# Opening of a three-block sequence model: x loaded half of its columns at a time on two queues, the norm's weight rows in a group of their own, and the norm's split parts made from the transposes in six banks

## The chip, the cores and the metric

One core of a Trainium2 chip (trn2) runs the kernel. The metric is the device time in microseconds (us), the median of several runs. A profile of one execution, taken by the hardware profiler, shows what each engine did: TensorE (PE, with its weight loads as PEld), VectorE (DVE), ScalarE (ACT), GpSimd (POOL), and SyncE (SP), which here only issues DMAs.

## The reference, cut to what matters

Three blocks in a row work on x of 512 tokens by 1024 features in float32. The change lies at the start of the first:

```python
def rmsnorm(x, w):
    xf = x.astype(jnp.float32)
    y = xf * lax.rsqrt(jnp.mean(xf * xf, axis=-1, keepdims=True) + EPS)
    return (y * w.astype(jnp.float32)).astype(x.dtype)

h = rmsnorm(x, norm_mix_w[l])
proj = h @ w_in[l]          # split into the inputs of an SSM and a gated delta-rule mixer
...
x = x + merged @ w_out[l]
h = rmsnorm(x, norm_ffn_w[l])
gate, up = jnp.split(h @ w_ffn_in[l], [FFN_HIDDEN], axis=-1)
x = x + (jax.nn.silu(gate) * up) @ w_ffn_down[l]
```

The other two blocks (attention and recurrent mixers, feed-forward networks) are not touched.

## The kernel before, in words

Data lie in two ways: FM tiles hold 128 features on the partitions and the 512 tokens along the free dimension, TM tiles hold 128 tokens on the partitions. x comes in TM from DRAM and is needed in FM, as eight tiles. A float32 product is made of three products of split parts (`mm3`, L215 to L218): a high part `wh` or `hi` that ScalarE casts (L194), and a low part `wl` or `lo`, the rest, that VectorE subtracts (L195). Weights come in pieces of 512 KB through three raw buffers (`wr`) on SP's queue (L210).

The opening does this. `setup_consts` (L95 on) makes masks and the identity on VectorE from two index tiles of GpSimd (`ident` at L109; L118 is the last that reads both index tiles), and zeros a tile (L127) that is stored four times into DRAM areas (`blocks`, 256 KB and a small rest each, L132 and L133). Its scratch are tiles of the tag `tmp`, of which there are six: two index tiles, two made from these, two for the masks; the zeros are the seventh and take the slot of the first. `first_block` then loads x with `load_fm` (eight banks of transposes, copied into FM tiles by VectorE and ScalarE in turn, L365), loads vectors of per-feature weights as rows and transposes them into columns (`columns`, L138), among them the norm's weight, and calls `norm`. For each of the eight feature blocks `norm` scales x by the norm's weight into a high part (ScalarE, L322) and a low part (VectorE, L323), squares x (ScalarE, L325) and adds the squares up (VectorE, L327). After the last, TensorE sums over features (L282, in `token_sums`), VectorE finds the reciprocal root (L180 to L189, copied into `r` at L330), and TensorE spreads it over the partitions (L293, in `spread`). The first products of the input projection (32 columns of `dt` and of gates in `lin_small`, then two pieces of 128 columns) start from the parts that lack the root, and are multiplied by it afterwards; all that follows uses the whole norm, made by `whole`.

The order in which each engine runs is not that of the code. A framework orders the instructions of each engine when the program is built, by its own estimate of when each is ready, and puts the waits in; on the chip an engine then goes through its list in that order. A slot of a tag is given out again when the last reader of the tile before is done. Each DMA signals one of eight semaphores in turn, one set for SP's and ACT's DMAs together and one for POOL's, so a DMA is not issued before the one eight places before it in its set has landed.

Of the kernel before, what the change touches and what calls it, by code (L numbers as in the profile page):

```python
# [11 lines left out]
F32 = mybir.dt.float32  # L12
# [4 lines left out]
AF = mybir.ActivationFunctionType  # L17
# [3 lines left out]
P = 128  # L21
# [11 lines left out]
class Env:  # L33
    """Pools, constants and the pieces that the blocks share.

    FM tiles hold features on partitions and the 512 tokens along the free
    dimension; TM tiles hold 128 tokens on partitions."""
# [14 lines left out]
    @contextmanager  # L52
    def on(self, stream):
        """Tiles inside come from the slots of a scan's stream ("a" or "b"): slots of one tag
        are given out in program order, so work that is to run side by side has its own."""
        kept, self.stream = self.stream, stream
        yield
        self.stream = kept
# [79 lines left out]
    def columns(self, parts):  # L138
        """Vectors whose elements belong to features, as columns: parts is a
        list of (name, AP of [rows, 128]); gives name -> [128, rows] APs."""  # L140
# [3 lines left out]
        def flush():  # L144
            rows = self.tmp()[:, :P]
            at = 0
            for _, ap, r in group:
                nc.gpsimd.dma_start(rows[at:at + r, :], ap)
                at += r
# [19 lines left out]
    def bcast_load(self, ap1d, n):  # L169
        """A vector of n elements, on every partition."""  # L170
# [4 lines left out]
    def rsqrt(self, ss, n, scale, eps):  # L175
        """(ss * scale + eps) ** -0.5 on a [128, n] piece; eps a number or such a piece."""
# [15 lines left out]
    def split(self, src, hi, lo):  # L192
        """src as the exact sum of two float32r parts."""
# [3 lines left out]
    def parts(self, src):  # L197
        """The two parts of src in tiles of their own."""
# [4 lines left out]
    def weights(self, w, k0, nk, c0, nf):  # L203
        """Rows k0*128.. (nk blocks) and columns c0..c0+nf of w [K, F], split."""
# [15 lines left out]
    def lin_fm(self, w, c0, ncols, h, epi, k0=0, nk=KB):  # L220
        """epi(i, psum) for each 128 columns of x @ w[:, c0:c0+ncols], FM."""
# [10 lines left out]
    def lin_tm(self, w, c0, h, epi, ncols=S):  # L232
        """epi(c, g, psum) for each 128 tokens and each 256 columns of x @ w[:, c0:c0+ncols], TM."""
# [17 lines left out]
    def lin_small(self, w, pieces, h):  # L251
        """The few columns of pieces, (first, number) each, FM: psum [columns, 512]."""
# [15 lines left out]
    def to_tm(self, fm, r0, nf):  # L268
        """Rows r0..r0+nf of an FM tile, TM: psum [128 tokens, 4, nf]."""
# [7 lines left out]
    def token_sums(self, acc):  # L277
        """acc: FM [128, 512] already summed over feature blocks; psum [128 tokens, 4] with the
        sums over all features."""
# [5 lines left out]
    def token_rstd(self, acc, scale, eps):  # L285
        """The reciprocal root of the sums of acc, in a psum bank, on all partitions."""
# [1618 lines left out]
```

## Time and profile before

| what | us |
|---|---|
| time, median of 3 runs | 3030.83 |
| lowest and highest run | 3030.61, 3033.38 |
| span of the profiled execution | 3028.6 |
| TensorE busy in it | 2947.4 (97%) |
| VectorE busy | 1735.4 (57%) |
| ScalarE busy | 1112.4 (37%) |

The span runs from the first to the last instruction of the profiled execution. What lies around it is not in the profile: the median of the runs is 2.2 us above this span. Busy time is that of matrix products on TensorE, of computing instructions on the others; the issue of a DMA is not counted. Idle time of an engine that does not hold up the others costs nothing.

### The profile page before, as it was taken

The page shows a single profiled execution, that of the slowest core. Times are in us where ns is not written, and L with a number is a line of the kernel's source. Part 1 is how long each engine was busy: PE and PEld are TensorE (multiplying, and loading weights), DVE is VectorE, ACT ScalarE, POOL GpSimd, SP SyncE. Part 2 cuts the span into 40 slices and gives each one's busy share as a digit, 9 for nine tenths or more (in the row PEclk, how much of TensorE's full clock was granted, in tenths as well). Part 3 has the DMA queues.
Part 4 walks back from the last instruction along what each step waited for, and adds up shares of the span by engine and source line. Part 5 has one row for each costly group of instructions (what it writes and reads, how often), then busy time and mean ns, then how long its engine had stood idle before and what let it go on. Part 6 is the DMA issues. An engine that isn't in the chain of part 4 may idle for free. (4 is left out here: it accounts for less than half of the span.)

```text
span 3028.6 us, 39369 instructions
## 1 busy us (share of the span) xinstructions
PE 2947.4 (97%) x15170; PEld 2430.1 (80%) x15170; DVE 1735.4 (57%) x3871; ACT 1112.4 (37%) x2076; POOL 46.9 (2%) x95
## 2 busy tenths in 40 slices
PE   6999999999999999999999999999999999999999
PEld 4778888888788886788978878888987978888887
DVE  6787737655655457977653564333757563553343
ACT  4435424433322233333253332222465553332221
POOL 1000000000000000000000000000000000000000
PEclk9999999999999998999999999999999999999999
DMA  5222233233445322222113423333321214333332
GB/s 125 78 58 77 60 96 98 68 97 98 139 144 162 91 84 85 71 59 58 34 32 87 131 83 92 98 97 102 118 70 57 63 44 131 98 91 96 99 91 90
DMA packets 481660, 269.06 MB, mean 89 GB/s; under 512 B 30607, under 2 KB 469073, under 8 KB 481473
## 3 DMA queue, kind: packets, MB, share of 16 engines
q1 hardware_dynamic: 445680, 255.67, 28.9%
q10 hardware_dynamic: 33920, 9.44, 1.3%
q0 software_dynamic: 1872, 1.43, 0.6%
q8 instruction: 120, 1.97, 0.3%
q14 instruction: 68, 0.55, 0.1%
HBM read 252.20 MB, written 14.16 MB: 88 GB/s over the span
## 5 line engine op out<-in xcount | busy, mean ns | idle before, releaser
L194 ACT CAST wh<-wr 128x1024 fp32r<-128x1024 f32 (+3 forms) x447 | 454.0, 1016 | 1293.0 <-PE pl L217 914.3
L216 PE MATMUL pl<-h,wh 128*128 128x512 f32 x2224 | 878.8, 395 | 10.0 <-DVE long L1186 4.6
L218 PE MATMUL pl<-h,wl 128*128 128x512 f32 x2224 | 875.7, 394 | 11.5 <-DVE wl L195 11.5
L217 PE MATMUL pl<-h,wh 128*128 128x512 f32 x2224 | 878.0, 395 | 1.0 <-DVE h L195 1.0
L195 DVE TENSOR_TENSOR wl<-wr,wh 128x1024 fp32r<-128x1024 f32 (+3 forms) x447 | 525.9, 1177 | 413.3 <-ACT wh L194 402.0
L216 PEld LDWEIGHTS pl<-h,wh 128*128 128x128 f32 x2224 | 419.8, 189 | 100.6 <-DVE long L1186 5.4
L218 PEld LDWEIGHTS pl<-h,wl 128*128 128x128 f32 x2224 | 419.2, 189 | 100.9 <-DVE wl L195 14.8
L217 PEld LDWEIGHTS pl<-h,wh 128*128 128x128 f32 x2224 | 419.5, 189 | 90.3 <-issue 3.5
L217 PE MATMUL pl<-long,wh 128*128 128x512 f32 x648 | 252.9, 390 | 0.2 <-DVE long L195 0.2
L216 PE MATMUL pl<-long,wh 128*128 128x512 f32 x648 | 253.1, 391 | 0.0
L218 PE MATMUL pl<-long,wl 128*128 128x512 f32 x648 | 253.0, 390 | 0.0
L543 DVE SCALAR_TENSOR_TENSOR long<-pl,long 128x512 f32<-128x512 f32 x72 | 49.8, 691 | 178.3 <-PE pl L218 178.3
L216 PEld LDWEIGHTS pl<-long,wh 128*128 128x128 f32 x648 | 121.7, 188 | 26.3 <-issue 1.0
L218 PEld LDWEIGHTS pl<-long,wl 128*128 128x128 f32 x648 | 121.7, 188 | 25.6 <-issue 0.3
L217 PEld LDWEIGHTS pl<-long,wh 128*128 128x128 f32 x648 | 121.7, 188 | 25.4 <-DVE long L195 0.7
L531 DVE TENSOR_TENSOR tmp<-tmp,pl 128x512 f32<-128x512 f32 x66 | 45.3, 686 | 149.2 <-PE pl L218 149.2
L216 PE MATMUL pl<-tmpa,wh 128*128 128x512 f32 (+1 forms) x304 | 120.1, 397 | 3.4 <-ACT tmpa L322 3.4
L217 PE MATMUL pl<-tmpb,wh 128*128 128x512 f32 (+1 forms) x304 | 120.9, 398 | 0.1
L218 PE MATMUL pl<-tmpa,wl 128*128 128x512 f32 (+1 forms) x304 | 120.2, 396 | 0.0
L216 PEld LDWEIGHTS pl<-tmpa,wh 128*128 128x128 f32 (+1 forms) x304 | 57.3, 189 | 16.8 <-ACT tmpa L322 4.0
L217 PEld LDWEIGHTS pl<-tmpb,wh 128*128 128x128 f32 (+1 forms) x304 | 57.4, 189 | 13.2 <-DVE tmpb L323 1.3
L218 PEld LDWEIGHTS pl<-tmpa,wl 128*128 128x128 f32 (+1 forms) x304 | 57.5, 189 | 13.0 <-issue 0.7
(772 smaller groups left out, 4034.5 us busy)
## 6 DMA issues: line engine op xcount, KB each, us to landing
wr<-in_w_in SPq DMA_DIRECT2D x169, 512.0 KB, 3.7
wr<-in_w_ffn_in SPq DMA_DIRECT2D x44, 512.0 KB, 4.0
wr<-in_ffn_w_gate SPq DMA_DIRECT2D x44, 512.0 KB
wr<-in_ffn_w_up SPq DMA_DIRECT2D x44, 512.0 KB, 3.8
wr<-in_ffn_w_down SPq DMA_DIRECT2D x32, 448.0 KB, 3.7
wr<-in_w_ada SPq DMA_DIRECT2D x24, 512.0 KB, 3.5
wr<-in_w_out SPq DMA_DIRECT2D x16, 512.0 KB, 3.9
wr<-in_ffn_w_down SPq DMA_DIRECT2D x16, 512.0 KB, 3.9
```

Source lines behind the costliest of these rows:

```text
L194: self.nc.scalar.copy(hi, src)
L195: self.nc.vector.tensor_tensor(lo, src, hi.bitcast(F32), ALU.subtract)
L216: mm(ps, wh, xh, start=first, stop=False)
L217: mm(ps, wh, xl, start=False, stop=False)
L218: mm(ps, wl, xh, start=False, stop=last)
L531: nc.vector.tensor_tensor(t1, t1, ps, ALU.mult)
L543: nc.vector.scalar_tensor_tensor(x[i], ps, scale, x[i], ALU.mult, ALU.add)
```

## The change

- `load_fm`, which loaded eight pieces of x on SP's queue, transposed them and copied the eight banks into FM tiles, is gone. `fetch_tm` loads the pieces half of the columns at a time, by turns on SP's and ACT's queue; the pieces of the first half are `tmp` tiles, those of the second `out` tiles (before: `tmpa` and `tmpb`).
- The norm's weight rows are a group of `columns` of their own, loaded on ACT's queue; the other groups stay on POOL's.
- `norm` is given these pieces and makes the transposes itself, in three pairs of PSUM banks by turns. High part, low part and squares are read from the bank, and VectorE copies the bank into the FM tile after that.

Comments were emptied too (left out here). After the change the lines in `norm` are L328 (transposes), L329 (high part), L330 (low part), L332 (squares), L335 (copy into the FM tile), L337 (sum of squares), L340 (`r`), and L364 the loads of x.

```diff
-    def columns(self, parts):
+    def columns(self, parts, queue=None):
...
-                nc.gpsimd.dma_start(rows[at:at + r, :], ap)
+                (queue or nc.gpsimd).dma_start(rows[at:at + r, :], ap)
...
-    def norm(self, x, gain):
+    def norm(self, x, gain, tm=None):
...
-            nc.scalar.activation(hi, x[k], AF.Copy, scale=col)
-            nc.vector.scalar_tensor_tensor(lo, x[k], col, hi.bitcast(F32), ALU.mult, ALU.subtract)
+            src = x[k] if tm is None else None
+            if src is None:
+                with self.on(("a", "b", "")[k % 3]):
+                    src = self.ps()
+                for c in range(NC4):
+                    nc.tensor.transpose(src[:, c * P:(c + 1) * P], tm[k // 4][c][:, (k % 4) * P:(k % 4 + 1) * P], self.ident)
+            nc.scalar.activation(hi, src, AF.Copy, scale=col)
+            nc.vector.scalar_tensor_tensor(lo, src, col, hi.bitcast(F32), ALU.mult, ALU.subtract)
             sq = self.tmp()
-            nc.scalar.activation(sq, x[k], AF.Square)
+            nc.scalar.activation(sq, src, AF.Square)
+            if tm is not None:
+                x.append(self.long())
+                nc.vector.tensor_copy(x[k], src)
...
-    def load_fm(self, src):
-        """[512, 1024] from DRAM as 8 FM tiles."""
-        nc = self.nc
-        tm = []
-        for c in range(NC4):
-            pair = []
-            for half in range(2):
-                with self.on("ab"[half]):
-                    t = self.tmp()
-                nc.sync.dma_start(t, src[c * P:(c + 1) * P, half * S:(half + 1) * S])
...
+    def fetch_tm(self, src):
+
+        halves = []
+        for half in range(2):
+            tiles = []
             for c in range(NC4):
...
+                t = self.out() if half else self.tmp()
+                (self.nc.sync, self.nc.scalar)[c % 2].dma_start(t, src[c * P:(c + 1) * P, half * S:(half + 1) * S])
+                tiles.append(t)
+            halves.append(tiles)
+        return halves
...
-    x = env.load_fm(a["x"][0])
-    cols = env.columns([
-        ("norm", vec("norm_mix_w")),
+    x, xtm = [], env.fetch_tm(a["x"][0])
+    cols = env.columns([("norm", vec("norm_mix_w"))], nc.scalar)
+    cols |= env.columns([
         ("conv_b", vec("ssm_conv_b")),
...
-    raw, rb, _, whole = env.norm(x, cols["norm"])
+    raw, rb, _, whole = env.norm(x, cols["norm"], xtm)
```

What stands on the engines, in the built programs. The start of SP's queue before (`wr` are weights, the first with 64-byte rows; `blocks` the stores of zeros):

```order
L356 DMA tmpa_162<-in_x 128x512
L356 DMA tmpb_164<-in_x 128x512
L356 DMA tmpa_166<-in_x 128x512
L356 DMA tmpb_168<-in_x 128x512
L356 DMA tmpa_170<-in_x 128x512
L356 DMA tmpb_172<-in_x 128x512
L356 DMA tmpa_174<-in_x 128x512
L356 DMA tmpb_176<-in_x 128x512
L260 DMA wr_365<-in_w_in 128x8x16 x2
L210 DMA wr_461<-in_w_in 128x8x128
L210 DMA wr_503<-in_w_in 128x8x128
L132 DMA blocks_106<-tmp_104 128x512
```

and in the changed program:

```order
L364 DMA out_170<-in_x 128x512
L364 DMA out_174<-in_x 128x512
L260 DMA wr_370<-in_w_in 128x8x16 x2
L210 DMA wr_466<-in_w_in 128x8x128
L210 DMA wr_508<-in_w_in 128x8x128
L210 DMA wr_614<-in_w_in 128x8x128
L210 DMA wr_654<-in_w_in 128x8x128
L364 DMA tmp_162<-in_x 128x512
L132 DMA blocks_106<-tmp_104 128x512
L133 DMA blocks_106<-tmp_104 4x128
L132 DMA blocks_109<-tmp_104 128x512
L133 DMA blocks_109<-tmp_104 4x128
```

Two tiles of the second half (`out`) now stand first, five loads of weights behind them, and the first tile of the first half (`tmp_162`) behind these; two more pairs of `blocks` stores and then `tmp_166`, the third quarter of the first half, follow the rows shown. On ACT's queue the order is two `out` tiles, the casts of the first two weight pieces, `tmp_164`, two small exponentials, `tmp_168`, and the norm's weight rows.

The start of VectorE's list before (from the end of its first zeros and ones):

```order
L1173 MEMSET starts_9212 128x4
L109 TENSOR_TENSOR ident_72<-tmp_80,tmp_81 128x128
L111 TENSOR_TENSOR upper_75<-tmp_81,tmp_80 128x128
L110 CAST identb_73<-ident_72 128x128
L112 TENSOR_TENSOR slower_76<-tmp_80,tmp_81 128x128
L113 TENSOR_TENSOR supper_77<-tmp_81,tmp_80 128x128
```

and at the same place in the changed program:

```order
L1173 MEMSET starts_9217 128x4
L195 TENSOR_TENSOR wl_372<-wr_370,wh_371 128x256
L195 TENSOR_TENSOR wl_468<-wr_466,wh_467 128x1024
L109 TENSOR_TENSOR ident_72<-tmp_80,tmp_81 128x128
L111 TENSOR_TENSOR upper_75<-tmp_81,tmp_80 128x128
L110 CAST identb_73<-ident_72 128x128
```

The low parts of the first two weight pieces (`wl_372`, `wl_468`) now stand ahead of `ident` and of the other masks.

TensorE around the transposes of the weight rows (L151) before; `pa_227` is the last bank of x, `pl` are the first products:

```order
L363 MATMUL pa_227<-ident_72,tmpb_172 128x128
L363 MATMUL pa_227<-ident_72,tmpb_176 128x128
L151 MATMUL pa_242<-ident_72,tmp_234 128x93
L151 MATMUL pa_248<-ident_72,tmp_246 128x96
L216 MATMUL pl_372<-tmpa_277,wh_366 32x512
L216 MATMUL pl_460<-tmpa_277,wh_462 128x512
L217 MATMUL pl_372<-tmpb_278,wh_366 32x512
```

and in the changed program, where the transposes of the norm's rows stand further ahead and these are those of the other rows:

```order
L218 MATMUL pl_377<-tmpa_239,wl_372 32x512
L217 MATMUL pl_465<-tmpb_227,wh_467 128x512
L151 MATMUL pa_191<-ident_72,tmp_184 128x85
L218 MATMUL pl_465<-tmpa_226,wl_468 128x512
L216 MATMUL pl_465<-tmpa_239,wh_467 128x512
L151 MATMUL pa_197<-ident_72,tmp_195 128x96
L328 MATMUL pa_255<-ident_72,tmp_162 128x128
L328 MATMUL pa_255<-ident_72,tmp_164 128x128
L328 MATMUL pa_255<-ident_72,tmp_166 128x128
L328 MATMUL pa_255<-ident_72,tmp_168 128x128
L328 MATMUL pa_297<-ident_72,out_170 128x128
L328 MATMUL pa_297<-ident_72,out_172 128x128
```

They stand in the middle of the first products, ahead of the transposes of the six later feature blocks save two that are made before (`pa_269`, `pa_283`). On POOL's queue the loads of these rows, which stood first after five small ones, now stand behind 18 loads of small vectors of this block and the later ones. The L282 products, which stood in the middle of the products of `pl_460`, now stand behind the last of them. From L293 on the orders of the computing engines are the same but for names, and for one weight piece's cast and low part, which stand ahead of the reciprocal root instead of behind it.

## Rows read from the trace of the kernel before

**Rows 1.** The page of the profile: the span, and TensorE's busy tenths in 40 equal slices of the span (75.7 us each).

```profile
span 3028.6 us, 39369 instructions
...
PE   6999999999999999999999999999999999999999
```

**Rows 2.** Busy time by stretch: the stretch, its length, busy us and instructions of each engine, granted clock of TensorE (share of full speed), share of the 16 DMA engines, GB/s.

```profile
34.00:38.00 4.00, 3.86 (x10) 1.56 (x11) 4.00 (x7) 4.00 (x8) 0.00 (x0) 0.63 1.05 395
...
60.00:80.00 20.00, 17.06 (x65) 12.28 (x63) 16.64 (x33) 12.35 (x22) 0.00 (x0) 0.83 0.18 52
80.00:100.00 20.00, 20.00 (x90) 16.54 (x89) 16.00 (x20) 8.23 (x11) 0.00 (x0) 1.00 0.32 90
```

**Rows 3.** The same view for the first 20 us.

```profile
0.00:4.00 4.00, 0.45 (x1) 0.18 (x1) 2.92 (x19) 0.00 (x0) 3.27 (x11) 1.00 0.51 160
4.00:16.00 12.00, 0.02 (x1) 0.02 (x1) 1.21 (x7) 0.00 (x0) 2.69 (x6) 1.00 0.81 61
16.00:18.00 2.00, 0.46 (x1) 0.16 (x1) 0.00 (x0) 0.00 (x0) 0.50 (x1) 1.00 0.82 204
```

**Rows 4.** DMA queues in two stretches, 4 to 8 us (first two lines) and 16 to 20 us (last line): packets, MB, share of 16 engines. q1 is SP's queue, q0 POOL's.

```profile
q0 software_dynamic: 24, 0.00, 84.8%
q1 hardware_dynamic: 107, 0.19, 13.0%
...
q1 hardware_dynamic: 1550, 0.73, 68.5%
```

**Rows 5.** Timeline of SP's queue: start us, duration us of the issue, engine, line, operation, out<-in.

```profile
5.92 4.73 SPq L356 DMA_DIRECT2D tmpa<-in_x  x1
...
13.99 3.15 SPq L260 DMA_DIRECT2D wr<-in_w_in  x2
17.18 4.68 SPq L210 DMA_DIRECT2D wr<-in_w_in  x2
...
24.77 0.63 SPq L132 DMA_DIRECT2D blocks<-tmp  x1
```

**Rows 6.** DMA issues of the first 50 us: out<-in, engine, count, KB each, median us from issue to landing.

```profile
spill<-long SPq DMA_DIRECT2D x8, 256.0 KB, 4.5
...
blocks<-tmp SPq DMA_DIRECT2D x4, 256.0 KB, 5.8
...
skip<-in_ssm_d POOLq DMA_DIRECT2D x2, 2.0 KB, 12.1
...
qkgain<-in_k_gain POOLq DMA_DIRECT2D x2, 0.2 KB, 6.2
...
tmp<-in_norm_ffn_w POOLq DMA_DIRECT2D x1, 4.0 KB, 4.4
...
tmp<-in_gdn_norm_w POOLq DMA_DIRECT2D x1, 0.5 KB, 2.8
```

**Rows 7.** Timeline of POOL: start us, us, and in brackets the idle time before it and what ended it.

```profile
4.62 0.53 POOL L148 DMA_DIRECT2D tmp<-in_norm_mix_w  x1
...
17.25 0.50 POOL L148 DMA_DIRECT2D tmp<-in_norm_ffn_w  x1 [5.59 <-DMA skip<-in_ssm_d]
```

**Rows 8.** Timeline of ScalarE (ACT) in the opening.

```profile
22.25 1.28 ACT L194 ACT_TABLE_LOAD   x1 [22.25 <-DMA wr<-in_w_in]
...
26.75 1.04 ACT L194 CAST wh<-wr 128x1024 fp32r<-128x1024 f32 x1 [2.21 <-DMA wr<-in_w_in]
...
32.26 0.24 ACT L153 COPY cols<-pa 128x93 f32<-128x93 f32 x1 [0.28 <-PE pa L151]
...
33.21 3.17 ACT L322 ACTIVATE tmpa<-long,cols 128x512 fp32r<-128x512 f32 x5
```

**Rows 9.** Timeline of VectorE (DVE) in the opening.

```profile
2.31 0.28 DVE L109 TENSOR_TENSOR ident<-tmp,tmp 128x128 f32<-128x128 int32 x1
...
3.77 0.28 DVE L118 TENSOR_TENSOR tmp<-tmp,tmp 128x128 int32<-128x128 int32 x1
...
4.77 0.48 DVE L127 MEMSET tmp<- 128x512 f32 x1
...
26.57 0.69 DVE L365 COPY long<-pa 128x512 f32<-128x512 f32 x1 [0.18 <-PE pa L363]
...
27.83 1.23 DVE L195 TENSOR_TENSOR wl<-wr,wh 128x1024 fp32r<-128x1024 f32 x1
...
33.97 2.74 DVE L323 SCALAR_TENSOR_TENSOR tmpb<-long,cols,tmpa 128x512 fp32r<-128x512 f32 x4 [0.25 <-ACT tmpa L322]
...
37.89 0.68 DVE L327 TENSOR_TENSOR tmp<-tmp,tmp 128x512 f32<-128x512 f32 x1
...
45.21 0.16 DVE L180 TENSOR_SCALAR s<-pa 128x4 f32<-128x4 f32 x1 [2.44 <-PE pa L282]
...
48.67 0.17 DVE L330 COPY r<-s 128x4 f32<-128x4 f32 x1
```

**Rows 10.** Timeline of TensorE (PE) in the opening.

```profile
24.48 1.12 PE L363 MATMUL pa<-ident,tmpa 128*128 128x128 f32 x4 [1.26 <-ACT long L365]
...
44.22 0.95 PE L282 MATMUL pa<-ones,tmp 128*128 128x1 f32 x8
...
48.89 1.16 PE L293 MATMUL pa<-ident,r 128*128 128x128 f32 x8 [0.89 <-DVE r L330]
```

More of the change, by code (lines that the diff above doesn't have):

```diff
@@ L345, in norm @@
         return raw, rb, r, whole
-    def load_fm(self, src):
-        nc = self.nc
-        tm = []
-        for c in range(NC4):
-            pair = []
-            for half in range(2):
-                with self.on("ab"[half]):
-                    t = self.tmp()
-                nc.sync.dma_start(t, src[c * P:(c + 1) * P, half * S:(half + 1) * S])
-                pair.append(t)
-            tm.append(pair)
-        x = []
-        for k in range(KB):
-            ps = self.ps()
-            for c in range(NC4):
-                nc.tensor.transpose(ps[:, c * P:(c + 1) * P], tm[c][k // 4][:, (k % 4) * P:(k % 4 + 1) * P], self.ident)
-            t = self.long()
-            (nc.scalar.copy if k % 2 else nc.vector.tensor_copy)(t, ps)
-            x.append(t)
-        return x
+    def fetch_tm(self, src):
+        halves = []
+        for half in range(2):
+            tiles = []
+            for c in range(NC4):
+                t = self.out() if half else self.tmp()
[3 more added lines that the diff above has]
+        return halves
     def spill(self, x):
```

## Prediction

> **What bounds the kernel now.** I read the page first: TensorE is busy nine tenths or more of every slice but the first, where it has six tenths [rows 1]. By stretch it is full from 80 us on, has 17.1 of 20 us just before, and next to nothing in the first 18 [rows 2, 3]. So the reader is to see that a gain or a loss in the opening goes to the end one for one, and nothing else in the change can. I take one instant as the measure: the start of L293, the product that spreads the norm's reciprocal root over the partitions, at 48.9 us [rows 10]. Everything that TensorE can do before it is done by then, before and after, and the orders of all engines behind it are the same; so its shift is the change of the time.
>
> What makes the opening long is the second thing to see. In the first 4 us the DMA engines moved 160 GB/s; from 4 to 16 us only 61 GB/s at a share of 0.81, then 204 [rows 3]. The share from 4 to 8 us is POOL's: 24 packets took 84.8% of 16 engines, 2.3 us each, beside 107 packets from SP [rows 4]. Those are the two loads of `skip` (4-byte elements), 12.1 us to landing [rows 6]. SP's seventh load of x needed 4.73 us for its issue in that time [rows 5]. The first weights landed at 22.25 us, the first 512 KB piece at 26.75, and the norm's columns were copied at 32.3 [rows 8]. From there the low parts and sums run to L282 at 44.2, and 4.7 us later L293 [rows 9, 10].
>
> **The change, part by part.** The two queues, the split of the columns and the six banks would fill waits if the order of the code were the order on the engines. It is not. The first half of x is put in `tmp` tiles, and all six of these hold the masks' scratch, so its loads wait for VectorE's set-up; the second half, in `out` tiles, goes first. VectorE's set-up (from `ident` on), at 2.31 us before [rows 9], now stands behind the low parts of the first two weight pieces. So nothing on the path moves until the first 512 KB weight piece lands; call that moment T.
>
> T. Ahead of and in it are 1.0 MB of x, 64 KB of small weights and 0.52 MB: 1.64 MB in all. By the bytes of the trace, 0.64 MB are moved by 4 us, 0.73 by 16 us, and the rest at 204 GB/s: 17.3 us [rows 3]. This is the value if the slow spell stays as it is. A lower bound takes the spell away: 1.0 MB behind the 0.64 at 204 GB/s, 8.9 us. The upper bound lets the 2,048 64-byte packets of the small weights wait for the spell's end: 1,550 packets took 68.5% of 4 us, 28 ns of one engine each [rows 4], so 3.6 us, and then the 4.5 us that lay between the two landings before [rows 8]: 24.1 us. I take 18.5, near the first, since most of the bytes are packets of x as before. The Trainium skill, page "DMA: Bandwidth & Descriptors", section "Issuing engines are not separate DMA queues", says that queues of several engines share the same 16 DMA engines and that a second one saves only issue time, which speaks against a gain from two queues; the share of 0.81 at 61 GB/s agrees that the engines and not the issue were taken, and by it T stays at 17.3.
>
> From T on, each step by a row of before:
> - ScalarE's cast 1.04 and VectorE's low part 1.23 [rows 8, 9]: `ident` starts at T+2.3.
> - From its start to L118, after which the first `tmp` tile is free, 1.7 us; to the end of L127's zeros 2.9 [rows 9]: the first half's first load is issued at T+4.0, the first store of `blocks` at T+5.2. Before, both lay under the load of x, where VectorE was busy 1.2 of 12 us [rows 3], and cost nothing; that cover is gone.
> - On SP two more weight pieces, that load and the four pairs of `blocks` stores now stand ahead of the third quarter of the half (`tmp_166`). A store of 256 KB landed after 5.8 us, a like transfer (`spill`) after 4.5 [rows 6]; the x rows of before are inside the spell, so I use `spill`. A DMA waits for the one eight before it: `tmp_166` goes at T+5.2+5.8 and lands at T+15.5; the last pair waits for the first x tile, T+8.5, and lands at T+14.3.
> - The other columns' rows need the tile that held the zeros, so POOL begins them at T+14.3. Six loads at 0.53 [rows 7]; the fourth lands 4.4 after its issue, the sixth 2.8 [rows 6]: T+20.3, some 5 us behind x. TensorE has their transposes in the middle of its first products, so it waits here with all that follows. Transposes 0.3, ScalarE's copy 0.24 [rows 8]: T+20.8.
> - The copies of x into FM tiles, which before lay in waits for x, now come with the norm's own work. VectorE has left 6 low parts at 0.69 (2.74/4), 8 copies at 0.69, 7 additions at 0.68 [rows 9] and five small operations at 0.16, as L180: 15.2 us, T+36.0. ScalarE's 14 activations at 0.63 (3.17/5) [rows 8] are 8.9. TensorE's 40 products at 0.222 (20 us for 90) [rows 2] and 16 transposes at 0.28 [rows 10] are 13.4 at the full clock; at the granted 0.63 of 34 to 38 us [rows 2], some 2 more. Both hide under VectorE, TensorE only just. Reading a bank instead of SBUF I cost at nothing: L365 read one, and took 0.69 as the others.
> - L282 to L293, 4.7 before [rows 10]; one more weight low part (1.23) stands ahead of it on VectorE, of which 0.95 runs under L282: 5.1.
>
> L293 comes at T+41.1: at 18.5, 59.6 us. Against 48.9 that is 10.7 us more. The profiled span of 3028.6 becomes 3039.3; the median of the runs, 3030.8, is 2.2 above that span, and becomes 3041.5, my prediction.
>
> **The rivals.** *Early weights, no loss that can be measured.* With ACT's queue beside SP's, x and the weights could take two turns to each of POOL's and move twice as much in the spell: 1.0 MB at 122 GB/s behind 4 us gives T = 12.2, L293 at 53.3, +4.4: 3035.2. The Trainium skill, page "DMA: Bandwidth & Descriptors", section "Queues, rings and completion order", has each DMA engine go round the queues by packets, by which this holds as long as both queues have work. Against it: ACT's queue has only two tiles of 256 KB, and then SP is alone again. POOL sets a floor: its loads wait for the one eight before, the second `skip` landed at 17.25 [rows 7]; the second `k_gain` load behind it, issued at an estimated 19, takes 6.2 [rows 6], then the column loads 1.6 and 4.4, and by the steps above L293 comes at 52.0, +3.1: 3033.9. This decides for "no difference" if T lies under 13.9 us.
>
> *Late weights.* T = 24.1, L293 at 65.2, +16.3: 3047.1. For it speaks how long the small packets took before (issue at 13.99, landing 22.25 [rows 5, 8]), against it that x stood ahead of them.
>
> *A gain.* If the change did what its words say, the first half of x and the norm's weights would land within the first 8 us and the columns be there at 20 to 23; then L293 could fall to 40 to 43 us, 3022 to 3025. Against it stands the order itself: `ident` behind the weights, the half behind `ident`. It would need `skip` to land 10 us sooner and T under 2 us.
>
> **How the numbers follow.** A measurement of this kernel tells 0.2%, 6.1 us, from no change. Forecast (T from 15 to 22, +7 to +14): 0.66. Early weights: 0.17, all in "same". Late weights or slower landings of the stores: 0.13. A gain: 0.04. So slower 0.79, same 0.17, faster 0.04. The forecast's own range is 3037 to 3045. For 8 in 10 I add most of the early case and the late one: 3034 to 3048; left out are the gain, the floor's lower edge and a T beyond 25.
>
> **What would show it.** In the changed profile: `ident` (L109) at 15 to 24 us instead of 2.31; the loads of `tmp` tiles on SP and ACT behind it; the first column load on POOL's queue waiting for `blocks`, at about 33; TensorE waiting at L151 to about 39; L282 at about 54, L293 at about 59; and from there on every row later by one amount. It is wrong if the set-up runs early after all, if the columns are there before x, or if VectorE's 15.2 us shrink because its copies fall into waits; it is wrong in size if T lies off 18.5, one for one.

## The result, and the profile after

The changed kernel takes 3049.4 us (median of 5 runs, 3047.7 to 3056.0) against 3030.8: 18.6 us more. The ratio of the means is 1.0067 (95% interval 1.0055 to 1.0078, which is 16.7 to 23.6 us). The forecast was slower, 3041.5 with 3034 to 3048: the right sign, 7.9 us too little, and outside the range. The profiled execution is one of the two slowest of the five, 3055.5 us with a span of 3053.5; what that costs in it is told below.

The page of the changed kernel, which answers to [rows 1]:

```profile
span 3053.5 us, 39380 instructions
...
PE   4999999999999999989999999999999999999999
```

The first slice has four tenths instead of six, two tenths of some 76 us: most of the loss lies in the opening. The first stretches, which answer to [rows 3] (length, busy us of PE, PEld, DVE, ACT and POOL, granted clock, DMA share, GB/s), and one behind L282:

```profile
0.00:4.00 4.00, 0.00 (x0) 0.00 (x0) 1.29 (x9) 0.00 (x0) 3.27 (x11) 1.00 0.45 124
4.00:16.00 12.00, 0.00 (x0) 0.00 (x0) 0.00 (x0) 0.00 (x0) 2.83 (x7) 1.00 0.97 57
16.00:18.00 2.00, 0.00 (x0) 0.00 (x0) 0.00 (x0) 0.20 (x1) 0.94 (x2) 1.00 0.85 41
18.00:22.00 4.00, 0.00 (x0) 0.00 (x0) 0.43 (x1) 1.49 (x2) 2.92 (x5) 1.00 1.00 243
...
58.00:70.00 12.00, 6.47 (x27) 5.53 (x28) 8.61 (x28) 3.55 (x8) 0.00 (x0) 0.58 0.39 111
```

VectorE does nothing from 4 to 16 us, where it finished the masks and the zeros before (1.21 us [rows 3]), and the DMA engines are full at 57 GB/s; even from 16 to 18 us they move 41 GB/s, not 204. The timeline of the opening, ScalarE first, then VectorE, SP's queue, POOL and TensorE:

```profile
17.80 1.28 ACT L194 ACT_TABLE_LOAD   x1 [17.80 <-DMA wr<-in_w_in]
22.29 1.04 ACT L194 CAST wh<-wr 128x1024 fp32r<-128x1024 f32 x1 [2.79 <-DMA wr<-in_w_in]
42.89 0.23 ACT L153 COPY cols<-pa 128x85 f32<-128x85 f32 x1 [3.28 <-PE pa L151]
...
24.51 0.28 DVE L109 TENSOR_TENSOR ident<-tmp,tmp 128x128 f32<-128x128 int32 x1
57.49 0.68 DVE L337 TENSOR_TENSOR tmp<-tmp,tmp 128x512 f32<-128x512 f32 x1
...
26.28 0.34 SPq L364 DMA_DIRECT2D tmp<-in_x  x1
27.45 0.34 SPq L132 DMA_DIRECT2D blocks<-tmp  x1
32.35 0.34 SPq L364 DMA_DIRECT2D tmp<-in_x  x1
...
35.10 0.52 POOL L148 DMA_DIRECT2D tmp<-in_ssm_conv_b  x1 [11.81 <-DMA tmp<-in_x]
...
31.70 1.51 PE L328 MATMUL pa<-ident,tmp 128*128 128x128 f32 x6 [31.70 <-DMA tmp<-in_x]
37.23 0.69 PE L328 MATMUL pa<-ident,tmp 128*128 128x128 f32 x2 [3.16 <-DMA tmp<-in_x]
58.32 1.02 PE L282 MATMUL pa<-ones,tmp 128*128 128x1 f32 x8 [0.94 <-DVE tmp L337]
63.08 2.05 PE L293 MATMUL pa<-ident,r 128*128 128x128 f32 x8 [3.73 <-DVE r L340]
```

T, the landing of the first 512 KB weight piece, is the start of the second cast: 22.29 us. It was 26.75 before [rows 8], so the weights do land sooner; but `ident` now hangs on them, at 24.51 instead of 2.31 [rows 9]. L293 starts at 63.08, 14.2 us later than before [rows 10].

What held T up is read from the DMA queues. From 8 to 16 us, the kernel before first, then the changed one (packets, MB, share of 16 engines; q0 is POOL's queue, q1 SP's):

```profile
q0 software_dynamic: 126, 0.03, 55.2%
q1 hardware_dynamic: 283, 0.52, 17.7%
```

```profile
q0 software_dynamic: 98, 0.02, 71.4%
q1 hardware_dynamic: 788, 0.05, 6.7%
```

The spell in which `skip` takes the engines is there in both: its loads land after 12.1 us before [rows 6] and after 11.0 in the changed kernel. Before, pieces of x stood in SP's queue then: 283 packets carried 0.52 MB. Now x's second half is in ahead of the spell, SP's queue has come to the small weights with 64-byte rows, and 788 packets carry 0.05 MB. By these packets 2.2 of SP's went through for each of POOL's before, and 8 now, but a tenth of the bytes.

The Trainium skill, page "DMA: Bandwidth & Descriptors", section "Queues, rings and completion order", has each DMA engine take turns between the queues it has work for, packet by packet. The trace agrees that SP's queue goes on beside the slow one, a few packets for each of POOL's. It doesn't show a fixed share: neither the packets (2.2 and 8, and 1.2 in e5 below) nor the bytes (some 4 KB before and 0.5 KB now) are the same for each of POOL's.

### The profile page after: what moved, and what is told of

It is laid out like the page before. It is cut to its first block, busy times and chain, and to the rows that moved or that the text cites. A ratio compares the mean times of both kernels' runs of the same rounds, so it can differ in the third digit from the quotient of the medians.

```text
span 3053.5 us, 39380 instructions
## 1 busy us (share of the span) xinstructions
PE 2955.1 (97%) x15171; PEld 2437.9 (80%) x15171; DVE 1737.8 (57%) x3875; ACT 1110.4 (36%) x2073; POOL 46.4 (2%) x94
## 5 line engine op out<-in xcount | busy, mean ns | idle before, releaser
L217 PEld LDWEIGHTS pl<-tmpb,wh 128*128 128x128 f32 (+1 forms) x304 | 57.5, 189 | 16.5 <-DVE tmpb L330 4.3
```

The costliest lines, as they stand in the source:

```text
L217: mm(ps, wh, xl, start=False, stop=False)
```

## The experiments

T and L293 are the starts of the cast and of the product in the profiled execution. The lag is how much later the last `sconv` step of the opening's stage (L623, at 127 us in the kernel before) starts than in the first profile of the kernel before. "More" is the median less that of the kernel before on the same chip (3031.4, 3030.5, 3029.3, 3030.2 and 3031.4 for e1 to e4, e5 to e8, e9 to e12, e13 and e14, e15 and e16).

| kernel | T | L293 | lag | median | more |
|---|---|---|---|---|---|
| before | 26.8 | 48.9 | 0 | 3030.8 | 0 |
| changed | 22.3 | 63.1 | 14.9 | 3049.4 | 18.6 |
| e1 changed, no slow `skip` | 14.0 | 53.3 | 6.3 | 3041.9 | 10.5 |
| e11 changed, half of it | 18.8 | 58.4 | 10.6 | 3046.2 | 16.9 |
| e6 queues, tiles of the change | 22.7 | 60.9 | 16.5 | 3049.3 | 18.8 |
| e5 queues, own tiles | 23.1 | 48.4 | -0.8 | 3030.9 | 0.4 |
| e10 norm's rows alone | 27.6 | 49.4 | 0.3 | 3035.7 | 6.4 |
| e7 banks alone | 24.1 | 48.1 | 0.4 | 3032.6 | 2.2 |
| e9 queues, own tiles, banks | 22.9 | 48.5 | 2.3 | 3035.8 | 6.4 |
| e3 all three, own tiles | 23.5 | 53.4 | 7.4 | 3041.8 | 10.4 |
| e4 before, delayed | 23.8 | 62.6 | 16.5 | 3047.1 | 15.7 |
| e13 before again | 26.2 | 49.1 | -0.4 | 3030.7 | 0.4 |
| e14 changed again | 22.9 | 62.1 | 14.8 | 3048.9 | 18.6 |
| e15 before, one DMA more | 26.8 | 49.7 | 0.9 | 3032.3 | 1.0 |
| e16 before, eight more | 25.7 | 47.7 | -1.4 | 3032.8 | 1.5 |
| e2 before, no slow `skip` | 17.9 | 39.4 | -5.7 | 3027.7 | -3.7 |
| e8 e5, no slow `skip` | 15.6 | 38.9 | -5.5 | 3026.6 | -3.9 |
| e12 e9, no slow `skip`, copies shared | 15.7 | 40.8 | -5.8 | 3025.5 | -3.8 |

In e9 two casts stand in one row that starts at 22.5; 22.9 is its first 0.4 us further. The 95% interval of a ratio is 0.0009 to 0.0015 to either side, so "more" is known to within 3 to 5 us: the 0.4 to 2.2 of e5, e7, e15 and e16 are hardly told from nothing.

### What sets T: the slow packets, in doses

e1 loads the 16 numbers of `skip` as a row on all partitions; e11 does that for one of the two loads.

```diff
+    every = env.bcast_load(a["ssm_d"], 16)
     for e in range(2):
-        nc.gpsimd.dma_start(skip[e * 64:(e + 1) * 64, :, None], dram_ap(a["ssm_d"], e, [[0, 64], [2, 8], [1, 1]]))
+        nc.vector.tensor_copy(skip[e * 64:(e + 1) * 64, :], every[e * 64:(e + 1) * 64, e:16:2])
```

> The changed kernel with the two loads of `skip` (4-byte elements on POOL's queue) replaced by one load of the 16 numbers as a row onto all partitions and two strided copies on VectorE. The orders of SP, TensorE and the set-up stay as in the changed kernel: `ident` still stands behind the low parts of the first two weight pieces. Theory 1 (the loss is the lateness of T, the landing of the first 512 KB weight piece, and T is late because the slow packets of `skip` hold the 16 DMA engines while SP's queue holds small packets): T falls from 22.3 to 8 to 12 us, and L293 comes 41 us after it, at 49 to 53; time 3031 to 3036. Rival 1 (the small 64-byte packets of the first weights are slow by themselves, or the 4-byte loads of q_gain and k_gain take the place of skip's): T stays above 17, L293 above 58; time 3042 or more. Rival 2 (T doesn't set the chain; the columns' rows do, over POOL's queue): T falls, but L293 does not follow at 41 us and stays above 56.

> The changed kernel with one of the two loads of `skip` replaced by the row load, so that about half of the slow packets are left. Theory 1 (T is set by when POOL's slow packets end, not by the bytes ahead of it): the spell ends at about 10 to 11 us instead of 16, T lies between the 14.0 us without and the 22.3 us with both, at 16.5 to 19.5; L293 39 to 41 us behind it, at 56 to 60. Rival (bytes: 1.64 MB at the rate of the stretch, which half a spell would raise as well, to 17.3 less 3): T at 14 to 15, as without any. Time by theory 1: 3043 to 3047.

Timelines of e1 and then of e11, ScalarE's second cast and L293, and e1's stretch from 4 to 16 us:

```profile
13.99 1.04 ACT L194 CAST wh<-wr 128x1024 fp32r<-128x1024 f32 x1 [2.65 <-DMA wr<-in_w_in]
...
53.33 2.04 PE L293 MATMUL pa<-ident,r 128*128 128x128 f32 x8 [3.73 <-DVE r L340]
```

```profile
4.00:16.00 12.00, 0.00 (x0) 0.00 (x0) 1.36 (x2) 2.73 (x3) 6.79 (x13) 1.00 1.09 196
```

```profile
18.75 1.04 ACT L194 CAST wh<-wr 128x1024 fp32r<-128x1024 f32 x1 [2.79 <-DMA wr<-in_w_in]
...
58.44 2.05 PE L293 MATMUL pa<-ident,r 128*128 128x128 f32 x8 [3.74 <-DVE r L340]
```

With none, one and both slow loads T is 14.0, 18.8 and 22.3, and L293 follows 39.3, 39.7 and 40.8 us behind. The spell sets T, and the chain behind T has nearly one length, as theory 1 of both runs said. T is 14.0 and not 8 to 12, though: without the spell the stretch moves 196 GB/s where the changed kernel moves 57, but the row loads and small weights are packets too (2,506 of 5,512 in e1 are under 512 bytes). And the loss stays: with T 12.8 us sooner than before, e1 is still 10.5 us slower than the kernel before, since `ident` waits for the weights all the same. The time was expected at 3031 to 3036, and is 3041.9; what is behind L293 costs more than the forecast had, which e4 and the last section of runs take up.

### What makes `ident` wait: the tiles

e5 is the kernel before with the pieces of x half-first on two queues, in `tmpa` and `tmpb` tiles; e6 is e5 with the tiles of the change.

```diff
+        for half in range(2):
+            for c in range(NC4):
+                with self.on("ab"[half]):       # e6: t = self.out() if half else self.tmp()
+                    t = self.tmp()
+                (nc.sync, nc.scalar)[c % 2].dma_start(t, src[c * P:(c + 1) * P, half * S:(half + 1) * S])
```

> The kernel before with only the first part of the change: x half of the columns first, by turns on SP's and ACT's queue, but in `tmpa` and `tmpb` tiles as before; copies into FM tiles, columns and norm as before. In the built program `ident` stays early and the four tiles of the first half come first. Theory 1 (two queues bring x in before `skip` takes the engines, as the `out` tiles landed 4.6 us after issue in the changed kernel; then the columns' rows on POOL's queue and T near 22 to 24 are the bound): x landed by 8 us, the columns copied at 24 to 28 instead of 32.3, L293 16.6 us after them, at 41 to 45; some of it lost again in the chains behind (as 4.5 of 10.4 us were in the kernel before without `skip`): time 3024 to 3029. Rival (a second queue saves only issue time: the engines are taken by `skip` either way): x lands no sooner than 14 us, L293 at 46 to 49.5; time 3029 to 3032.

> The kernel of the run before this (two queues, halves) with the one line on the tiles as in the change: `tmp` tiles for the first half, `out` for the second. Copies, columns and norm stay as in the kernel before the change. In the built program the bad order is back: `ident` behind the low parts of the first two weight pieces, the first half's loads behind five weight loads and the set-up. Theory 1 (the choice of tiles alone makes the loss): T at 20 to 24, `ident` 2.3 us later, L293 at 57 to 64; time 3040 to 3048. Rival (the loss is in the banks and in the columns' own group, which are not here): L293 below 52; time 3035 or less.

One line is between them, and 18.4 us. The order of e6 has `ident` behind the weights' low parts (at 24.92 us), that of e5 has it at 2.31. So the choice of `tmp` and `out` tiles is what put the set-up on the path; with the two queues it gives as much as the whole change. The parts don't add up, though: in the changed kernel the same line is worth 8.2 us (18.6 against the 10.4 of e3 below). And the agreement with the whole change is half luck (the time is 1 us above theory 1's range): L293 is at 60.9, 2.2 us sooner than in the changed kernel, and 4.5 us are lost behind it, where TensorE waits 3.5, 2.2, 1.8 and 1.5 us for VectorE and ScalarE. In e6, e2 and e8 the built order behind L293 differs from before (casts and low parts of weights come later), so their lags don't compare one for one with L293.

e5 misses its expectation: nothing is gained. Its timeline, TensorE, then ScalarE:

```profile
6.16 1.54 PE L361 MATMUL pa<-ident,tmpa 128*128 128x128 f32 x6 [0.48 <-DMA tmpa<-in_x]
24.63 1.97 PE L361 MATMUL pa<-ident,tmpa 128*128 128x128 f32 x8 [16.93 <-ACT long L363]
...
23.05 1.04 ACT L194 CAST wh<-wr 128x1024 fp32r<-128x1024 f32 x1 [0.23 <-DMA wr<-in_w_in]
24.00 0.58 ACT L363 COPY long<-pa 128x512 f32<-128x512 f32 x1
```

The first half of x is transposed from 5 to 8 us (its last piece in the kernel before at 20.8); but ScalarE copies every second bank, these copies stand behind the casts of the first weights in its list, and TensorE waits 16.93 us for a bank. What one wait lost, the next gained. The rival's time and L293 came out, for another reason than the rival's.

The second half of x is not in by then. In the spell, from 8 to 16 us, its packets still stand in both queues (q10 is ScalarE's), and fewer of them go through than in either kernel above:

```profile
q0 software_dynamic: 65, 0.01, 59.3%
q10 hardware_dynamic: 81, 0.16, 6.1%
q1 hardware_dynamic: 81, 0.14, 5.2%
```

### The other two parts, and all three with their own tiles

e7 takes the parts from the banks and leaves loads and columns as before; e10 takes only the norm's rows on ScalarE's queue; e9 is e5 with the banks; e3 is the changed kernel with the tiles of e5.

```diff
 # e10, in the kernel before; e9 is the changed kernel without this line's group and with the edit of e3
+    cols = env.columns([("norm", vec("norm_mix_w"))], nc.scalar)
 # e3, in the changed kernel
-                t = self.out() if half else self.tmp()
+                with self.on("ab"[half]):
+                    t = self.tmp()
```

> The changed kernel with the pieces of x in `tmpa` and `tmpb` tiles, as before the change, instead of `tmp` and `out`: two queues, halves of the columns, the norm's rows on their own and the six banks are kept. In the built program `ident` then stands ahead of the weights' low parts again, the pieces of the first half come first on SP's queue, and the columns' rows stand early on POOL's. Theory 1 (the loss comes from x's loads behind the set-up scratch and the set-up behind the weights): `ident` at about 2.3 us, x landed by 8, the columns by 25; T stays near 22 because `skip` is still there, VectorE's two low parts and 15.2 us of work follow it, L282 to L293 5.1, so L293 comes at about 45, 4 us before that of the kernel before; time 3026 to 3029. Rival (the loss comes from the making of the parts out of the banks, with the copies on VectorE, or from the columns' transposes inside the first products): L293 above 53; time 3035 or more.

> The kernel before with only the third part of the change: x loaded as before on SP's queue, the columns as before in two groups on POOL's queue, and `norm` making the parts, the squares and the copies from the transposes in three pairs of banks. Theory 1 (making the parts from the banks costs: VectorE's copies come with the norm's work, and TensorE has nothing left between L282 and L293, so that its granted clock falls): from the first columns' copy to L293 24 us as in the run with own tiles, instead of 16.6; the columns come earlier than at 32.3 as they don't wait for the transposes of x, at 25 to 29; L293 at 49 to 53, and 2 to 3 us more behind it at the low clock: time 3032 to 3038. Rival (the banks save the copies' waits, as the change says): L293 at 42 to 46; time 3024 to 3028.

> The kernel before with only the second part of the change: the norm's weight rows as a group of their own on ScalarE's queue. In the built program their load stands between the first two casts of weights. Theory 1 (issued with the first cast, at 22 to 24 us, they land 5 us later, no sooner than the columns were there before): norm's columns copied at 29 to 33, L293 16.6 us later at 46 to 50; time 3028 to 3033. Rival (its transposes and the other group's inside the first products cost as in the run with own tiles): L293 at 51 to 55; time 3036 to 3041.

> The changed kernel with x in `tmpa` and `tmpb` tiles, and with the norm's weight rows back in the first group of columns on POOL's queue: two queues and banks stay, the second part of the change is undone. It differs from the run with own tiles by the norm's rows alone. Theory 1 (in that run the norm's rows were issued on ScalarE's queue behind the first casts of weights, at 23.56 us, and landed at 29: a loss of its own): the first columns are copied at 24 to 26, L293 23 us later at 47 to 49, time 3030 to 3034. Rival (two queues and banks together lose by themselves): L293 at 52 or later; time 3038 to 3042.

ScalarE's queue and TensorE in e3, and in e7:

```profile
23.56 0.54 ACTq L148 DMA_DIRECT2D tmp<-in_norm_mix_w  x1
...
29.09 0.27 PE L151 MATMUL pa<-ident,tmp 8*128 8x8 f32 x1 [8.78 <-DMA tmp<-in_norm_mix_w]
53.40 2.05 PE L293 MATMUL pa<-ident,r 128*128 128x128 f32 x8 [3.75 <-DVE r L340]
```

```profile
25.17 0.22 ACT L153 COPY cols<-pa 128x93 f32<-128x93 f32 x1
...
48.07 2.05 PE L293 MATMUL pa<-ident,r 128*128 128x128 f32 x8 [3.74 <-DVE r L340]
```

e3 was expected at 45 for L293 and 3026 to 3029, and came at 53.4 and 3041.8, as its rival had it. Two things are in that, and the rival named one of them. The rows of the norm, which were to come first, are issued by ScalarE behind its first cast, at 23.56, and land 5.5 us later. And from the first columns on the banks need 22.9 us to L293 (e7, 25.17 to 48.07) where the copied x needed 16.6 [rows 8, 10]. Most likely that is VectorE's copies, which come with the norm's work now: VectorE is busy 17.4 of the 18.1 us from the columns to L282, some 5 of them with the eight copies. In e7 the columns are there 7 us sooner and this is used up: +2.2 us. e9, which differs from e3 by the norm's rows alone, has L293 at 48.5: the 4.9 us between them are the rows' lateness. Its time is 2 us above what was expected. e10 has L293 where it was expected and is 6.4 us slower all the same, 2.7 above its expected range; all ten of its runs (3032.6 to 3036.8) lie above the median of the kernel before on that chip, 3029.3. Neither theory has that.

### Whether a shift of L293 is the change of the time

e4 puts 76 dependent small copies behind the root; e13 and e14 are the kernel before and the changed kernel once more; e15 and e16 add one and eight DMAs that nobody reads.

```diff
 # e4
+            for _ in range(38):
+                nc.vector.tensor_copy(other, r)
+                nc.vector.tensor_copy(r, other)
 # e15, with 8 in e16
+    for _ in range(1):
+        nc.scalar.dma_start(env.const([8, 32], base="extra"), vec("norm_mix_w")[:, :32])
```

> The kernel before with a chain of 76 dependent copies of 128x4 on VectorE behind the first norm's reciprocal root (`r`), about 14 to 16 us by the 0.17 to 0.2 us of such a copy; nothing else changes. It shifts L293 and leaves the orders behind it alone. Theory 1 (a shift of L293 is the change of the time, one for one): the time rises by the shift of L293 in the trace, to within 1.5 us: about 3045 to 3046.5 for 15 us. Rival (a later opening also costs time in later stages, by TensorE's granted clock or by what the weights run into): the time rises by 2 to 8 us more than L293 shifts, and the lag grows in the recurrent stage between 1,200 and 1,400 us as it did in the changed kernel.

> The kernel before once more, for a second profile of it. Theory 1 (behind the first 130 us the time scatters by drops of TensorE's granted clock behind short idle spots, which come in some executions of any kernel): against the first profile of the kernel before, the lag grows by 0 to 5 us somewhere behind 500 us, in steps, where the granted clock differs. Rival (the growth of the lag behind 500 us belongs to kernels with a later opening): the lag stays within 1 us from 130 us to the end.

> The changed kernel once more, for a second profile. Both theories: T at 22 to 23, L293 at 62 to 64, a lag of 15 us at 130 us. Theory 1: behind that the lag grows by 0 to 5 us, without the steps of 4.6, 2 and 2 us between 1,233 and 1,420 us that the first profile has; median 3047 to 3050. Rival: the same steps of 8 us at the same places; median 3050 or more.

> The kernel before with one more small DMA on ScalarE's queue at the start (8 pieces of 32 numbers into a tile that nobody reads); the orders of all engines are otherwise the same. All kernels so far with the norm's rows on ScalarE's queue waited 3.2 to 3.5 us for the loads of `blocks` between 525 and 710 us, all others 1.4 to 2.2. Theory 1 (SP's and ScalarE's DMAs signal one set of eight semaphores in turn; one DMA more shifts all that follow by one place, so that far behind the opening other DMAs are waited for): that wait is 3.2 to 3.5 us here too, and the time rises by 1 to 4 us: 3031 to 3034. Rival (it comes from the columns' own group, its tiles or its later landing): the wait stays at 1.4 to 2.2 us; time 3029 to 3031.

> As the run before this, with eight such DMAs, a whole turn of the set. Theory 1: all that follow have their old places again, and the wait for the loads of `blocks` between 525 and 710 us is 1.4 to 2.2 us; time 3029 to 3031. Rival (any added DMA delays the rest): 3.2 us or more; time 3031 or more.

In e4 L293 follows L282 after 21.2 us instead of 4.7, a delay of 16.6, and the time rises by 15.7: one for one within 1 us. (Its L282 is 2.9 us sooner than in the kernel before, though nothing ahead of it differs: so much does the opening scatter from profile to profile. By the shift of L293 itself, 13.7, which the expectation named, the time rises by 2.0 more, and the two theories aren't told apart.) L293 and a stretch behind it:

```profile
62.55 2.07 PE L293 MATMUL pa<-ident,r 128*128 128x128 f32 x8 [17.39 <-DVE r L336]
```

```profile
62.50:73.00 10.50, 8.97 (x28) 7.28 (x29) 7.26 (x18) 6.26 (x11) 0.00 (x0) 0.52 0.00 1
```

After 17 us without products TensorE starts again at a granted clock of 0.52, close to the lower of its two levels (1.2 GHz): L293 takes 2.07 us instead of 1.16 [rows 10], and the lag grows from 13.7 at L293 to 16.5 at 127 us. In the changed kernel TensorE idles for 3.7 us there, L293 takes 2.05, and the lag goes from 14.2 to 14.9.

Behind 500 us there is more. One place, the stretch of 8 us ahead of it and the one with it: the kernel before (first profile), the kernel before again (1.5 us earlier there), the changed kernel, and the changed kernel again (second stretch):

```profile
1226.00:1234.00 8.00, 6.28 (x37) 4.82 (x34) 6.58 (x17) 3.50 (x7) 0.21 (x1) 1.00 0.26 68
1234.00:1242.00 8.00, 8.00 (x43) 6.86 (x43) 6.68 (x32) 1.63 (x2) 0.32 (x1) 1.00 0.15 39
```

```profile
1224.50:1232.50 8.00, 6.31 (x37) 4.80 (x34) 6.58 (x16) 3.56 (x7) 0.18 (x1) 1.00 0.26 68
1232.50:1240.50 8.00, 8.00 (x29) 6.94 (x29) 4.29 (x17) 1.63 (x2) 0.34 (x1) 0.58 0.00 0
```

```profile
1242.00:1250.00 8.00, 6.26 (x37) 4.84 (x34) 6.58 (x17) 3.51 (x7) 0.23 (x1) 1.00 0.26 68
1250.00:1258.00 8.00, 8.00 (x29) 6.89 (x29) 4.34 (x19) 1.63 (x2) 0.29 (x1) 0.58 0.00 0
```

```profile
1253.00:1261.00 8.00, 8.00 (x45) 6.92 (x45) 6.50 (x32) 1.63 (x2) 0.53 (x1) 1.00 0.09 18
```

The same work with the same idle share ahead of it (6.26 to 6.31 us busy of 8) is followed by a clock of 1.00 in one execution and of 0.58 in another, and the first two fences are one and the same program. Here and at two places up to 1,420 us that costs 4.6, 2 and 2 us: the changed kernel's first profile has all three (lag 16.0 to 24.1), its second none, and the kernel before has none in its first profile and all three in its second. That part, 8 us of the profiled execution's 25, is scatter and not the change: theory 1 of e13 and e14, though the lag grows by more behind 130 us than the 0 to 5 us of both (7.6 and 6.2).

Not all of the growth is scatter. TensorE's waits for a load of `blocks`, 525 to 710 us in the kernel before, in the like stretches of the changed kernel, of e15 and of e16:

```profile
PE pa L464 <- DMA tmpa<-blocks: 1.6, 2, 1.0
```

```profile
PE pa L464 <- DMA tmpa<-blocks: 3.2, 2, 2.0
```

```profile
PE pa L464 <- DMA tmpa<-blocks: 3.5, 2, 2.1
```

```profile
PE pa L464 <- DMA tmpa<-blocks: 2.0, 2, 1.1
```

Every kernel with the norm's rows on ScalarE's queue waits 3.2 to 3.5 us there, every other but e15 1.4 to 2.2. The orders of the engines are the same in that stage. One unused DMA more in the set of SP's and ScalarE's queues gives 3.5, eight give 2.0: with eight semaphores given out in turn, one DMA more moves all later ones by a place, and a whole turn moves none. So the second part of the change reaches 500 us ahead.

What that costs stands in the lag of VectorE's instructions across this stage (500 to 610 us in the kernel before). It grows by at most 0.1 us in the ten profiles without the added DMA, by 0.6 to 0.9 in the changed kernel, e3 and e10, and by 2.3 to 2.4 in the changed kernel again, e1, e11 and e15. In these four TensorE's clock falls behind the longer wait, in the others not. The changed kernel, then the changed kernel again:

```profile
570.00:580.00 10.00, 7.92 (x56) 6.74 (x55) 2.50 (x4) 4.03 (x7) 0.00 (x0) 1.00 0.50 132
570.00:580.00 10.00, 7.76 (x41) 6.33 (x40) 2.71 (x4) 2.56 (x5) 0.00 (x0) 0.83 0.51 137
```

The times don't confirm it: e15 is 1.0 us slower than the kernel before (ratio 1.0002, 0.9993 to 1.0011), and e16, with the short wait, 1.5 (1.0008, 0.9998 to 1.0018), against an expectation of no change.

### A kernel that beats both

> The kernel before with the same edit of `skip`, and nothing else. Theory 1: the slow spell from 4 to 16 us goes, x (2.1 MB) and the first weights land at 160 to 230 GB/s, T falls from 26.75 to 12 to 16 us, and L293 follows at T+22.1 as before: 34 to 38 us instead of 48.9; time 3015 to 3021. Rival (the spell is not skip's alone; other element loads of POOL take its place): T above 22, L293 within 4 us of 48.9; time 3027 to 3031. Rival 2 (the columns' rows on POOL's queue or VectorE become the bound): T falls to under 16, but L293 stays above 42; time 3024 or more.

> The kernel before with two queues and halves in `tmpa` and `tmpb` tiles, and with the row load of `skip`. Theory 1 (without the slow packets x lands by 5 to 7 us and the weights by 9 to 14; then the columns' rows on POOL's queue, some 18 to 19 us, are the bound): L293 16.6 us behind the columns, at 33 to 38; of these 11 to 16 us the chains behind it (decays of the state-space mixer, low parts of the weights) take back 4 to 6: time 3020 to 3025. Rival (the chains behind take back all beyond what the kernel before gained without `skip`): L293 below 38, but time 3026 to 3029.

> The run with two queues and banks, with the row load of `skip`, and with the copies of x out of the banks shared by VectorE and ScalarE in turn. Theory 1 (what limits the opening then is the columns' rows at 16 to 17 us, T at 15 to 16 and VectorE's 13 us of work for the norm, 2.7 less than with all copies): the first columns copied at 17 to 18.5, L282 at 31 to 33, L293 at 36 to 38; TensorE starts again at the low clock behind it, 2 to 3 us; time 3019 to 3024. Rival (the chains behind L293 take back all but 5 us, as in the two runs without `skip`): time 3025 to 3028.

All three take the slow `skip` away; e12 is e9 with that edit and with `(nc.scalar.copy if k % 2 else nc.vector.tensor_copy)(x[k], src)` for the copies. e2 moves L293 by 9.5 us and keeps 3.7 in the time, e8 10.0 and 3.9; both end below their expectations' gains, and TensorE then waits behind L293 for VectorE's decays and low parts and a cast of ScalarE's in the order built there (in e8 2.2, 2.2, 2.2 and 1.9 us). e12 brings L293 to 40.8, not 36 to 38, and its time is the rival's. The shared copies didn't shorten the way from the columns to L282 (18.05 us, 18.1 in e7), and the way from there to L293 is 1 us longer, as two low parts of weights stand inside the chain to the root. The ratio of e12 is 0.9989 (0.9980 to 0.9998), that of e2 0.9990 (0.9981 to 0.9999), that of e8 0.9993 (0.9983 to 1.0002). So e12 and e2 beat the kernel before by 0.1%; the three aren't told from one another.

## Why the prediction was right in sign and short in size

**What bounds, and the order.** Right. The loss is in the opening, `ident` stood at T+2.2 (told: T+2.3), and e6 against e5 shows that the tiles put it there.

**From T on.** Right, nearly step by step: first half's first load T+4.0 (told 4.0), first store of `blocks` T+5.2 (5.2), `tmp_166` landed T+14.9 (15.5), POOL's column loads T+12.8 (14.3; by the profile they waited for a load of x, not for a store of `blocks` as told), columns copied by T+20.8 (20.8), VectorE's last addition ended at T+35.9 (36.0), L293 at T+40.8 (41.1). Doses of the spell keep that length at 39.3 to 40.8. Two sums are off without weight: the small weights are 0.13 MB and not 64 KB (2,048 rows of 64 bytes), 0.3 us in T, and the step from L282 to L293 adds up to 5.0, not 5.1 (measured: 4.8).

**T.** This step failed: told 18.5, measured 22.3 (22.9 in the second profile). The prediction had both mechanisms and chose the wrong one, "near the first, since most of the bytes are packets of x as before". The x of `out` tiles was in ahead of the spell (4.6 us from issue to landing on SP's queue), so what stood in SP's queue during the spell was the small weights' 64-byte packets. They landed at 17.80, and the 512 KB piece 4.5 us behind them, which was written down as the upper bound, 24.1, and given 0.13. Bytes ahead of T at a rate were the wrong measure in another way too: 1.64 MB were counted, and by 22 us some 2.2 MB had moved, since later weights and POOL's loads moved beside them. T is 3.5 of the 7.9 us that were missing: L293 came at 63.1, told 59.6. (In e5 T is 23.1 by another way: x's second half was still in the queues during the spell, and the small weights came behind it, at 21.1.)

**One for one.** "Its shift is the change of the time" is the other failed step, and the other 4.4 us: a shift of 14.2 became 18.6. For a delay alone it is right within 1 us by the delay put in (e4: 16.6 and 15.7), 2.0 us short by L293 itself. Shown of the 4.4 are 0.7 by 127 us, from L293 and what follows at the lower clock, and 0.6 (first profile) to 2.4 (second) at the loads of `blocks` that the added DMA lengthens. The prediction looked at the orders behind L293, which are the same, and not at the turn of the semaphores, which isn't. The rest, 1 to 3 us, is not settled, and is no more than the interval of the measured change leaves open. Taking the lag at 127 us from the change of the median, the six profiles of kernels with the norm's rows on ScalarE's queue leave 3.0 to 6.3 us, the eleven others -0.8 to 4.1: the second part seems to cost more behind the opening than what was found, but one profile's opening scatters by 3 us, and the added DMA alone didn't show it (e15: 0.1).

**The rivals.** Early weights: T fell, but to 22.3, not 12.2. Late weights was the nearest, 3047.1. The gain needed `skip` gone and the set-up off the weights; with both (e12) it is 4 us, not the 6 to 9 that were written. L293 is there at 40.8, inside the 40 to 43 of that rival, but its shift of -8.1 is a lag of -5.8 at 127 us and -3.8 in the time: the rest is lost behind it.

## What to carry to other kernels

A tile's tag is an order: before a load is moved to the front, ask which tiles hold its slots and who frees them; here one line of tags cost 18 us beside the two queues alone and 8 us in the whole change, and the other parts gained nothing: queues and banks cost 6 us together, the rows on ScalarE's queue 6 alone, all three 10. While a queue of tiny elements is running, don't reckon the others by bytes at a rate, and leave the tiny loads out first: 16 numbers loaded as a row gained 3.7 us in the kernel before and 8.1 in the changed one. A load on a computing engine's queue starts when that engine gets there (the norm's rows in e3 at 23.56 us), and one DMA more or less shifts the semaphores of all that follow.

## What the runs showed of the hardware that was not expected

- In the spell of `skip`'s 4-byte elements, SP's queue got 283 packets through in 8 us where most were of 2 KB (0.52 MB), 788 where they were of 64 bytes (0.05 MB), and 81 of mostly 2 KB where ScalarE's queue had as many (0.14 MB): neither the number nor the bytes were fixed.
- The granted clock fell to 0.58 behind the same short idle spot in some executions of a program and stayed at 1.00 in others; falls at three such places make 8 us, 0.3% of the time, and the runs of one kernel spread by as much.
- One unused DMA of 1 KB at the start lengthened a wait 550 us later from 1.6 to 3.5 us, eight of them left it at 2.0. Behind the longer wait the clock fell in four of seven profiles, behind the shorter in none of eleven.
